# A second set of 16 value tiles of the last up projection made as seven block products

## The chip, the cores and the metric

The kernel runs on one core of one Trainium2 chip. The metric is the device time of one execution in microseconds; lower is better. Before the change three runs gave 2538.35 to 2538.91 us, with a median of 2538.77 us. One more execution was recorded by the profiler, and it took 2537.81 us; its span, from the first to the last instruction of the program, is 2535.6 us. All rows quoted below are of that execution, and times in rows are counted from the start of its span.

## The reference

The computation is a two-layer encoder on 16 learned meta tokens and 256 input tokens, with 2048 channels, in float32. Cut to what matters here, each layer is

```python
h = _rmsnorm(h_stream, norm_mix[i])
proj = h @ w_in[i]                                  # q, k, v, f, ga, gf
merged = g_attn * (attn @ w_attn_br[i]) + g_four * (fourier @ w_four[i])
h_stream = h_stream + merged @ w_out[i]

h2 = _rmsnorm(h_stream, norm_ffn[i])
up = h2 @ w_up[i]                                   # 2048 -> 2 * 5632
u_gate = _dwconv3_centred(up[..., :D_FF], w_conv[i], b_conv[i])
u_val = up[..., D_FF:]
h_stream = h_stream + (jax.nn.silu(u_gate) * u_val) @ w_down[i]
```

Only the 256 input tokens of the last layer are returned. The change is in the second half of layer two: in how a part of `u_val` is computed, and in the layer-two work that prepares its weights.

## The kernel before, in words

**Chunks.** Every weight matrix goes through TensorE (the matmul engine) in chunks of 512 KB: a tile of 128 partitions by 1024 float32 values, holding 4 blocks of 128 input channels by 256 output channels. A chunk is loaded by a transfer of the SP queue into a `raw` buffer (`load_raw`, line 244). It is then split in two parts that TensorE multiplies one after the other: ScalarE (ACT) makes the rounded part `wh` (line 280), and VectorE (DVE) makes the rest, `wl = raw - wh` (line 282). There are three `wh` and three `wl` buffers and four `raw` buffers; in the last stage every third load goes into one of two more (`raw5`), so that there are six. `next_split` keeps the splits two chunks ahead of TensorE. The chunks, in the order in which TensorE needs them, are one long list that is written out when the program is built.

**A group.** `group` takes the four chunks of a pair of channel tiles (2 x 128 output channels against 2048 input channels) and makes three matmuls for each block: `wh` with the rounded input, `wh` with the input's rest, `wl` with the rounded input (lines 343 to 345). For the value half of the last layer the two inputs are put side by side in one matmul of 512 columns, followed by one of 256 (lines 339 and 340, output `ps_uv`). For the gate half (`ps_ug`) the three matmuls have 258 columns. After every second block `step` is called, which lets work that waits in the background go on by one step. A chunk of a group has eight blocks and so four steps.

**The last stage.** In layer two the 22 pairs of the up projection are walked in the order `UP_ORDER`. For each pair comes the gate group (`ug`), its convolution and silu (`conv_gate`, lines 1210 to 1216), and then the value group (`uv`), whose result is put together on ACT and DVE (`v`, lines 1408 and 1409) and multiplied with the gate. Each activation of the first 40 channel tiles goes to the down projection, which is itself made as two sets (of 12 and 8 quarter products, `SETS`) of seven block products, with the scheme of Strassen and Winograd: sums of activation blocks times sums of weight blocks, seven products where the plain scheme has eight. The last four channel tiles (`t`) go through a plain down projection at the end.

**Products.** A product takes one chunk and makes six matmuls of 512 columns (line 1366, output `ps_p`). The generator `products` is drawn on between the chunks of the groups: the table `DUE` says how many products are to be done when t chunks of the last stage have been taken, with straight lines between its points. Between t = 8 and t = 152 it spreads 196 products. Their left operands (`opnd`) are sums of blocks, made on DVE and split on ACT and DVE by `make` and `split_unit` up to two units of three ahead; a finished product is handed out of PSUM by ACT or DVE (`hand_out`, `add`).

**One value set as products already.** Eight of the 22 pairs (`VPAIRS`, 16 channel tiles) have no `uv` group. Their values are made ahead by the first 56 products: block products of the scaled token stream with sums of the value weights. The results stand in `vR` with tokens on the partitions, and when such a pair's turn comes, four matmuls turn them (`ps_vr`, line 1399) and DVE multiplies them with the gate (line 1401).

**Sums of weights.** Four of the seven products need sums of weight blocks. For both the value set and the down projection these are made in layer one, between the feed-forward chunks, by `prepare`: transfers of the POOL queue bring weights into SBUF (`wi`), DVE adds (line 505), transfers of the POOL queue write the sums to DRAM (`fv`, `ft`, line 506). This runs at about 560 to 1260 us.

**What stands around the change.** The branch stage of layer two walks `BRANCH_ORDER` in two halves: gates `ga` and `gf`, the fourier and attention projections `s` and `a`, and after each half the eight groups of the output projection (`ps_o`). POOL's queue is in order, and its instruction for the root in the norm (`tok`, line 484) stands in it between that stage and the last one.

Of the kernel before, what the change touches and what calls it, by code (L numbers as in the profile page):

```python
# [16 lines left out]
P = 128  # L17
# [23 lines left out]
def _sets():  # L41
    up, prods, home, q0 = [], [], {}, 0
    for n in SETS:
        up += VFIRST if q0 == 0 else [q0 + i + j * n // 2 for i in range(n // 2) for j in range(2)]
        prods += _seven(1 + len(prods) // (7 * SETS[0]), q0, n)
        for k in range(n):
            home[2 * q0 + k], home[2 * q0 + n + k] = q0 + k, NQ + q0 + k
        q0 += n
    return up + list(range(NQ, FT // MG)), _seven(0, 0, NV) + prods, home
# [8 lines left out]
VPAIRS = [4, 10, 5, 11, 6, 7, 8, 9]  # L58
VFIRST = [0, 1, 2, 3] + VPAIRS[4:] + VPAIRS[:4]
UP_ORDER, PRODUCTS, HOME = _sets()  # L60
FIRSTS = [sum(SETS[:i]) for i in range(len(SETS))]
BEGIN = {(0, 0)} | {(i + 1, q) for i, q in enumerate(FIRSTS)}
END = {(0, NV - 1)} | {(i + 1, q + n - 1) for i, (q, n) in enumerate(zip(FIRSTS, SETS))}
DUE = ((0, 0), (8, 0), (34, 42), (50, 56), (64, 76), (66, 76), (112, 140), (128, 152), (130, 152), (144, 180), (150, 196), (152, 196))
# [94 lines left out]
def encoder_kernel(ctx, tc, xT, params, consts, bmat, cfold, csign, w_fl, w_f64c, w_in, w_abr, w_four, w_f64, w_out, w_up, w_down, w_vn, w_dn, w_dt, out):  # L159
# [8 lines left out]
    fv = dram.tile([4, NV, P, CW, MG * P], F32, name="fv")  # L168
# [38 lines left out]
    vprods = {0: w_vn[0, 0:NV], 1: w_vn[0, NV:KT], 2: w_vn[1, NV:KT], 3: fv[3], 4: fv[0], 5: fv[1], 6: fv[2]}  # L207
    pchunks = [((prods if s else vprods)[p][k], CW) for s, p, k in PRODUCTS]
# [7 lines left out]
    for key, chs in order:  # L216
        for j, ch in enumerate(chs):
# [4 lines left out]
            if n:  # L222
                mix[key, j] = n
                for s, p, k in PRODUCTS[done:done + n]:
                    if p in (3, 4, 5, 6):
                        summed[len(chunks)] = (s > 0, (3, 0, 1, 2)[p - 3], k)
                    chunks.append(pchunks[done])
                    done += 1
# [45 lines left out]
    def split_w(i, a, b, parts="hl"):  # L274
        if i not in splits:
            splits[i] = tuple(wp.tile([P, CW, MG * P], F32R, tag=t, name=f"{t}{i}") for t in ("wh", "wl"))
        h, lo = splits[i]
        r = raws[i]
# [11 lines left out]

    def step(force=False):
        for s in shadow:
# [211 lines left out]
    def prepare(pool):  # L504
# [5 lines left out]
        for f, wd, nq in ((fv, w_vn, NV), (ft, w_dn, NQ)):  # L510
            for k in range(nq):
                sums += [(wd[h, nq * e + k], (f, q, k)) for h, e, q in ((0, 0, 0), (1, 0, 2), (1, 1, 1), (0, 1, 3))]
# [10 lines left out]
        def sum_up(held, n, f, q, k):  # L523
# [5 lines left out]
            ready_sums.add((f is ft, q, k))  # L529

        for jobs, ahead, work in ((folds, 2, lambda h, n, to: fold(h, n, to)), (sums, 4, lambda h, n, to: sum_up(h, n, *to))):
            held = {}
            for n in range(len(jobs) + ahead):
# [8 lines left out]
                yield left  # L542

# [26 lines left out]

    xr = lambda lo: (lambda kt: (xH[:, kt, lo:T], xL[:, kt, lo:T]))
# [949 lines left out]
```

## Time and profile before

| what | value |
|---|---|
| median of the runs (range) | 2538.77 us (2538.35 to 2538.91) |
| profiled execution | 2537.81 us |
| its span | 2535.6 us |
| PE (TensorE matmul) busy | 2526.2 us, 100% of the span |
| DVE busy | 1952.5 us, 77% |
| ACT busy | 1317.9 us, 52% |
| POOL busy | 174.5 us, 7% |
| moved by DMA | 660.71 MB, mean 261 GB/s |

PE is the matmul row, and its busy time is the union of matmuls that overlap in the pipeline; what one costs is seen from the distance between starts. PEld is the load of weights into TensorE, which runs beside it. In a row of a group, the numbers behind the bar are the total and the mean duration of one instruction, then the idle time of the engine just before. In a row of a stretch of time there is, after its length, the busy time of each engine with the count of its instructions, then the granted TensorE clock, the busy share of the DMA engines and what they moved in GB/s. In a row of the timeline the first number is the start, the second the duration, and in brackets stands the idle time before it and what ended it. In a row of the DMA issues the last number is the median time from issue to landing.

### The profile page before, as it was taken

The numbers are of one execution on the slowest core, as the hardware profiler recorded it, in microseconds if no ns is written. First come the engines' busy times: TensorE is split into PE (matmuls) and PEld (weight loads), VectorE is DVE, ScalarE is ACT, GpSimd is POOL, SyncE is SP. The second block draws the span as 40 slices with busy tenths as digits, with TensorE's granted clock in tenths as the row PEclk, the third lists the DMA queues.
The fourth block names the chain that finished last, engine by engine and source line by source line (L and its number), as shares of the span: only waits on it lengthen the run. The fifth ranks groups of instructions, "written<-read, shape, count | busy, mean of one in ns | idle before, by whom it ended". The sixth has DMA issues, their size and how long they took to land.

```text
span 2535.6 us, 47924 instructions
## 1 busy us (share of the span) xinstructions
PE 2526.2 (100%) x18992; PEld 2445.7 (96%) x18992; DVE 1952.5 (77%) x3113; ACT 1317.9 (52%) x1893; POOL 174.5 (7%) x329
## 2 busy tenths in 40 slices
PE   9999999999999999999999999999999999999999
PEld 8999999999999999999999999999988999888987
DVE  7687866778878667888768787666778778777787
ACT  5455534454444334444445555444666566666565
POOL 0000000012212222222200000000000000000000
PEclk9999999999999999999999999999999999999999
DMA  6444555569999999999975645555578777877787
GB/s 238 164 157 161 188 181 186 186 240 372 388 336 377 398 381 366 389 382 379 386 267 187 194 142 187 193 195 195 184 252 268 246 251 252 264 262 265 240 269 256
DMA packets 186450, 660.71 MB, mean 261 GB/s; under 512 B 21217, under 2 KB 26465, under 8 KB 186225
## 3 DMA queue, kind: packets, MB, share of 16 engines
q1 hardware_dynamic: 143312, 504.51, 57.5%
q0 software_dynamic: 41472, 151.01, 15.8%
q8 instruction: 149, 2.44, 0.4%
q10 hardware_dynamic: 1440, 2.13, 0.2%
q14 instruction: 77, 0.62, 0.1%
HBM read 577.19 MB, written 77.59 MB: 258 GB/s over the span
## 4 chain that ended last, share of the span: by engine, by line
PE 99%; DMA 1%; DVE 0%; ACT 0%; SPq 0%; issue 0%; POOL 0%; ACTq 0%
PE ps_p L1366 11%; PE ps_ug L344 7%; PE ps_ug L345 7%; PE ps_ug L343 7%; PE ps_uv L339 4%; PE ps_d L343 4%; PE ps_uv L344 3%; PE ps_d L344 3%; PE ps_d L345 3%; PE ps_uv L345 3%; PE ps_uv L343 3%; PE ps_gf L344 2%; PE ps_ga L344 2%; PE ps_gf L345 2%; PE ps_o L344 2%; PE ps_o L345 2%
## 5 line engine op out<-in xcount | busy, mean ns | idle before, releaser
L282 DVE TENSOR_TENSOR wl<-raw,wh 128x1024 fp32r<-128x1024 f32 (+1 forms) x937 | 1129.2, 1217 | 445.9 <-ACT wh L280 437.7
L280 ACT CAST wh<-raw 128x1024 fp32r<-128x1024 f32 (+1 forms) x937 | 974.8, 1045 | 918.9 <-PE ps_ug L344 200.8
L344 PE MATMUL ps_ug<-xHL,wh 128*128 128x272 f32 (+1 forms) x1408 | 402.0, 286 | 0.0
L345 PE MATMUL ps_ug<-xHL,wl 128*128 128x272 f32 (+1 forms) x1408 | 401.4, 285 | 0.0
L343 PE MATMUL ps_ug<-xHL,wh 128*128 128x272 f32 (+1 forms) x1408 | 400.9, 285 | 0.0
L343 PEld LDWEIGHTS ps_ug<-xHL,wh 128*128 128x128 f32 x1408 | 264.6, 188 | 3.5
L344 PEld LDWEIGHTS ps_ug<-xHL,wh 128*128 128x128 f32 x1408 | 264.7, 188 | 3.3
L345 PEld LDWEIGHTS ps_ug<-xHL,wl 128*128 128x128 f32 x1408 | 264.7, 188 | 0.0
L344 PE MATMUL ps_uv<-xHL,wh 128*128 128x272 f32 x704 | 203.3, 289 | 0.0
L343 PE MATMUL ps_d<-gHL,wh 128*128 128x272 f32 x704 | 203.1, 288 | 0.0
L344 PE MATMUL ps_d<-gHL,wh 128*128 128x272 f32 x704 | 203.0, 288 | 0.0
L345 PE MATMUL ps_d<-gHL,wl 128*128 128x272 f32 x704 | 202.6, 288 | 0.0
L345 PE MATMUL ps_uv<-xHL,wl 128*128 128x272 f32 x704 | 202.6, 288 | 0.0
L343 PE MATMUL ps_uv<-xHL,wh 128*128 128x272 f32 x704 | 202.3, 287 | 0.0
L1366 PE MATMUL ps_p<-wh,opnd 128*128 128x512 f32 x688 | 188.7, 395 | 0.0
L339 PE MATMUL ps_uv<-xHL,wh 128*128 128x512 f32 x448 | 159.7, 395 | 0.0
L343 PE MATMUL ps_ga<-xHL,wh 128*128 128x272 f32 (+1 forms) x512 | 147.9, 289 | 0.0
L505 DVE TENSOR_TENSOR wi<-wi,wi 128x512 f32<-128x512 f32 x224 | 146.9, 685 | 0.0
L343 PE MATMUL ps_gf<-xHL,wh 128*128 128x272 f32 (+1 forms) x512 | 146.8, 287 | 0.0
L344 PE MATMUL ps_gf<-xHL,wh 128*128 128x272 f32 (+1 forms) x512 | 146.1, 285 | 0.0
L344 PE MATMUL ps_ga<-xHL,wh 128*128 128x272 f32 (+1 forms) x512 | 146.1, 285 | 0.0
L344 PE MATMUL ps_o<-mL,wh 128*128 128x272 f32 (+1 forms) x512 | 146.0, 285 | 0.0
(375 smaller groups left out, 6044.0 us busy)
## 6 DMA issues: line engine op xcount, KB each, us to landing
raw<-in_w_up SPq DMA_DIRECT2D x320, 512.0 KB, 5.3
raw<-in_w_in SPq DMA_DIRECT2D x191, 512.0 KB, 3.5
raw<-in_w_down SPq DMA_DIRECT2D x88, 512.0 KB, 7.0
wi<-in_w_dn POOLq DMA_DIRECT2D x80, 512.0 KB, 9.6
ft<-wi POOLq DMA_DIRECT2D x80, 512.0 KB, 8.0
raw<-ft SPq DMA_DIRECT2D x80, 512.0 KB, 4.5
raw<-in_w_out SPq DMA_DIRECT2D x64, 512.0 KB, 3.5
raw<-in_w_dn SPq DMA_DIRECT2D x60, 512.0 KB, 4.6
```

The lines of the kernel that those rows point to most:

```text
L280: nc.scalar.copy(h[:, a:b], r[:, a:b])
L282: nc.vector.tensor_tensor(lo[:, a:b], r[:, a:b], h[:, a:b].bitcast(F32), op=ALU.subtract)
L339: nc.tensor.matmul(o2, h[:, c, sl], ab, start=kt == 0, stop=False)
L343: nc.tensor.matmul(o, h[:, c, sl], a, start=kt == 0, stop=False)
L344: nc.tensor.matmul(o, h[:, c, sl], b, start=False, stop=False)
L345: nc.tensor.matmul(o, lo[:, c, sl], a, start=False, stop=kt == nk - 1)
L505: tt = lambda *v, **kw: tc.keep_in_program_order(nc.vector.tensor_tensor(*v, **kw))
L1366: nc.tensor.matmul(ps[h], x, w[:, 512 * h:512 * h + 512], start=fresh and (s_, q) in BEGIN and first, stop=(s_, q) in END and end, skip_gr ...
```

## The change

A second set of eight pairs (16 channel tiles) loses its `uv` groups and is made by 56 products, as the first one is. The sets are `VSETS`; products of the last stage become 252 instead of 196, over 120 chunks instead of 152, with a new `UP_ORDER` and a new `DUE`. The results of the second set get four buffers of their own (`late..`), which are used again for the split tail activations (`tails`).

The second set's weight sums aren't made by `prepare`. They are made by `weight_sums` in layer two, from the fifth entry of the first half of the branch stage on, one transfer for every 15 steps, 32 in all. For each of four sums and each of four pieces of 1 MB there is one transfer from DRAM to DRAM on POOL's queue that copies the first operand, and later one that adds the second operand to it in DRAM (`accum_op=ALU.add`). In the built program a copy has 16 rows of 16,384 values and an adding transfer 256 rows of 1,024 values. Ahead of each, POOL copies one column of the newest `wl` (`tick`), so that the transfer isn't issued before DVE has come that far. The four pieces of a sum are issued as copy, copy, add, copy, add, copy, add, add.

The memory set aside for the descriptors of POOL's transfers is set to 8192.

```diff
-DUE = ((0, 0), (8, 0), (34, 42), (50, 56), (64, 76), (66, 76), (112, 140), (128, 152), (130, 152), (144, 180), (150, 196), (152, 196))
+VSETS = ([8, 9, 10, 11, 4, 5, 6, 7], [14, 18, 15, 19, 12, 16, 13, 17])
+VPAIRS = {i: (s, c) for s, v in enumerate(VSETS) for c, i in enumerate(v)}
+PRODUCTS = [v for s in range(len(VSETS)) for v in _seven(s, 0, NV)] + [v for i, n in enumerate(SETS) for v in _seven(len(VSETS) + i, FIRSTS[i], n)]
+UP_ORDER = [0, 1, 2, 3] + [i for v in VSETS for i in v[4:] + v[:4]] + list(range(NQ, FT // MG))
+DUE = ((0, 0), (7, 0), (43, 96), (62, 112), (64, 112), (98, 196), (100, 196), (118, 252), (120, 252))
...
+    slow = [0, None, 0]
+
     def step(force=False):
+        if not force and slow[1] and slow[2]:
+            slow[0] -= 1
+            if slow[0] <= 0:
+                slow[0] = slow[2]
+                if next(slow[1], None) is None:
+                    slow[1] = None
...
+    def weight_sums():
+        rows = lambda ap: ap.rearrange("k p c m -> (k p) (c m)")
+
+        def issue(out_, s, **kw):
+            tick = small.tile([P, 1], F32, tag="tick", name="tick", bufs=1)
+            tc.keep_in_program_order(nc.gpsimd.tensor_copy(tick, st["wl"][:, 0, 0:1].bitcast(F32)))
+            tc.keep_in_program_order(nc.gpsimd.dma_start(out_, s, **kw))
+
+        for s_ in range(1, len(VSETS)):
+            dst = lambda q, j: rows(fv[s_][q, 2 * j:2 * j + 2])
+            w = lambda h, k, j: rows(w_vn[s_, h, NV * k + 2 * j:NV * k + 2 * j + 2])
+            kinds = ((0, lambda j: w(0, 0, j), lambda j: w(1, 0, j)),
+                     (1, lambda j: dst(0, j), lambda j: w(1, 1, j)),
+                     (2, lambda j: w(1, 1, j), lambda j: w(1, 0, j)),
+                     (3, lambda j: w(0, 1, j), lambda j: dst(1, j)))
+            for q, base, more in kinds:
+                for j in range(NV // 2 + 1):
+                    if j < NV // 2:
+                        issue(dst(q, j), base(j))
+                        yield 1
+                    if j:
+                        issue(dst(q, j - 1), more(j - 1), accum_op=ALU.add, max_dma_last_dim=4096)
+                        ready_sums.update((s_, q, 2 * j - 2 + k) for k in range(2))
+                        yield 1
...
-                for kind, i in BRANCH_ORDER[half]:
+                for n_, (kind, i) in enumerate(BRANCH_ORDER[half]):
+                    if last and (half or n_ >= 4):
+                        slow[2] = 15
...
-                vR = [own[:, a:a + 8].rearrange("p k t -> p (k t)") for a in (SETS[0], NQ + SETS[0] - (X1 - X0))]
+                flat = lambda t_: t_.rearrange("p k t -> p (k t)")
+                vR = [[[flat(own[:, a + 4 * c:a + 4 * c + 4]) for c in range(2)] for a in (SETS[0], NQ + SETS[0] - (X1 - X0))],
+                      [[flat(fp.tile([P, 4, SEQ], F32, tag=f"late{h}{c}", name="vR")) for c in range(2)] for h in range(2)]]
...
-                tH = fp.tile([P, NT, SEQ], F32R, name="tH")
-                tL = fp.tile([P, NT, SEQ], F32R, name="tL")
+                tails = []
...
+                            if not tails:
+                                tails += [fp.tile([P, NT, SEQ], F32R, tag=f"late0{c}", name=f"t{c}") for c in range(2)]
...
-    nc = _bacc.Bacc("TRN2", target_bir_lowering=False, num_devices=1)
+    nc = _bacc.Bacc("TRN2", target_bir_lowering=False, num_devices=1, dynamic_dma_scratch_size=8192)
```

More of the change, by code (lines that the diff above doesn't have):

```diff
@@ L167, in encoder_kernel @@
     ft = dram.tile([4, NQ, P, CW, MG * P], F32, name="ft")
[L168 removed]
+    fv = [dram.tile([4, NV, P, CW, MG * P], F32, name=f"fv{i}") for i in range(len(VSETS))]
     IN_F, IN_K, IN_V, IN_Q, IN_GA, IN_GF = 6, 4, 5, 0, 10, 18
@@ L1295, in encoder_kernel @@
                 made = {}
+                live = {(s_, c): (6, 8)[c] for s_ in range(len(VSETS)) for c in range(2)}
                 def make(s_, p, k, n):
-                    if s_ == 0:
+                    if s_ < len(VSETS):
                         s = vs[:, k:k + n]
@@ L1328, in encoder_kernel @@
                 whole, used = {(0, k) for k in range(NV)}, [0, 0]
+                vmade = sum(s_ < len(VSETS) for (s_, _), _ in units)
                 def make_ahead():
@@ L1332, in make_ahead @@
                         (s_, p), qs = units[used[1]]
-                        if not whole.issuperset((min(s_, 1), q) for q in qs):
+                        if not whole.issuperset((s_ >= len(VSETS), q) for q in qs):
                             break
```

66 lines of the change are left out of this document (32 added, 34 removed).

## The prediction

> **What bounds the kernel now.** I read the page first, then the waits of TensorE, then the busy time of each engine by stretches.
>
> ```profile
> span 2535.6 us, 47924 instructions
> PE 2526.2 (100%) x18992; PEld 2445.7 (96%) x18992; DVE 1952.5 (77%) x3113; ACT 1317.9 (52%) x1893; POOL 174.5 (7%) x329
> ...
> GB/s 238 164 157 161 188 181 186 186 240 372 388 336 377 398 381 366 389 382 379 386 267 187 194 142 187 193 195 195 184 252 268 246 251 252 264 262 265 240 269 256
> ...
> PE 99%; DMA 1%; DVE 0%; ACT 0%; SPq 0%; issue 0%; POOL 0%; ACTq 0%
> ```
>
> PE is busy all the time and makes up 99% of the chain that ended last. A busy PE could still be slow, so I asked what its matmuls waited for from 560 us to the end. The answer is one row:
>
> ```profile
> PE ps_uv L340 <- DVE wl L282: 0.3, 1, 0.3
> ```
>
> So the order of matmuls runs at TensorE's own pace; fewer columns are worth their whole time, and nothing else is, unless a feeder gets late. The feeders by stretch (layer-one preparation; the part of layer two's branch stage that the change uses; three parts of the last stage):
>
> ```profile
> core 0: us, PE busy (x) PEld busy (x) DVE busy (x) ACT busy (x) POOL busy (x), PEclk, DMA share, GB/s
> 560.00:1260.00 700.00, 700.00 (x5585) 700.00 (x5584) 553.85 (x848) 298.72 (x371) 144.80 (x272) 1.00 1.00 378
> 1495.00:1825.00 330.00, 330.00 (x2761) 330.00 (x2760) 234.37 (x410) 167.41 (x262) 0.00 (x0) 1.00 0.56 189
> ...
> 1875.00:2150.00 275.00, 275.00 (x1775) 249.81 (x1774) 219.89 (x288) 172.10 (x219) 0.00 (x0) 1.00 0.78 256
> 2150.00:2420.00 270.00, 270.00 (x1645) 240.89 (x1645) 207.33 (x259) 162.47 (x203) 0.00 (x0) 1.00 0.77 256
> 2420.00:2500.00 80.00, 80.00 (x424) 68.24 (x423) 70.77 (x90) 54.06 (x69) 0.00 (x0) 1.00 0.84 281
> ```
>
> The granted clock is 1.00 throughout. DVE is at 77 to 80% of the last stage, and at 88% (70.77 of 80) in its densest part, still without a wait of PE.
>
> **TensorE's part of the sum.** The timeline of PE around a product, a value chunk, and a set of transposes:
>
> ```profile
> 1870.18 1.09 PE L1366 MATMUL ps_p<-wh,opnd 128*128 128x512 f32 x4
> ...
> 1871.58 0.40 PE L339 MATMUL ps_uv<-xHL,wh 128*128 128x512 f32 x1
> ...
> 1874.37 0.39 PE L1366 MATMUL ps_p<-wh,xHL 128*128 128x512 f32 x1
> ```
>
> ```profile
> 1984.22 0.60 PE L1399 MATMUL ps_vr<-cst,act 128*128 128x128 f32 x4
> ...
> 1986.05 0.28 PE L343 MATMUL ps_ug<-xHL,wh 128*128 128x258 f32 x1
> ```
>
> A product takes 1871.58 - 1870.18 = 1.40 us. A value chunk takes 1874.37 - 1871.58 = 2.79 us. Four transposes and one product take 1986.05 - 1984.22 = 1.83 us, so the transposes cost 0.43. Removed: 8 pairs x 4 chunks x 2.79 = 89.3 us. Added: 56 x 1.40 = 78.4 us, and 8 x 0.43 = 3.4 us. The balance is -7.5 us; with 2.80 a value chunk it is -7.8. I take -7.6. In the built program TensorE's order is the same as before up to the eighth chunk of the last stage, so nothing else moves.
>
> **The splits and DVE.** The last stage has 372 chunks instead of 348 (24 more). A cast and its split, and how closely DVE can start one after the other:
>
> ```profile
> 1630.16 1.05 ACT L280 CAST wh<-raw 128x1024 fp32r<-128x1024 f32 x1 [1.81 <-PE ps_o L344]
> 1633.03 1.05 ACT L280 CAST wh<-raw 128x1024 fp32r<-128x1024 f32 x1 [1.83 <-PE ps_o L344]
> ```
>
> ```profile
> 1634.12 1.22 DVE L282 TENSOR_TENSOR wl<-raw,wh 128x1024 fp32r<-128x1024 f32 x1 [1.65 <-ACT wh L280]
> ```
>
> ```profile
> 1905.43 1.22 DVE L282 TENSOR_TENSOR wl<-raw,wh 128x1024 fp32r<-128x1024 f32 x1
> 1906.57 0.48 DVE L1214 SCALAR_TENSOR_TENSOR cv<-u,prm,cv 128x256 f32<-128x256 f32 x1
> 1906.96 1.22 DVE L282 TENSOR_TENSOR wl<-raw,wh 128x1024 fp32r<-128x1024 f32 x1
> ```
>
> A split holds DVE for 1.14 us (1906.57 - 1905.43), 0.08 less than its duration; I take 0.08 off every DVE duration. The other durations:
>
> ```profile
> L1289 DVE SCALAR_TENSOR_TENSOR res<-ps_p,sgn,res 128x512 f32<-128x512 f32 (+1 forms) x29 | 20.8, 735 | 0.2 <-PE ps_p L1442 0.2
> L1409 DVE TENSOR_TENSOR v<-v,ps_uv 128x256 f32<-128x256 f32 x28 | 11.6, 416 | 0.0
> L1224 DVE TENSOR_TENSOR opnd<-vs,opnd 128x384 fp32r<-128x384 f32 (+1 forms) x12 | 6.0, 508 | 0.0
> L1347 DVE TENSOR_TENSOR act<-act,ps_p 128x512 f32<-128x512 f32 x6 | 3.9, 682 | 0.0
> L1303 DVE TENSOR_TENSOR vs<-XT 128x384 f32<-128x384 f32 (+1 forms) x6 | 3.0, 512 | 2.6 <-ACT XT L1276 2.5
> ```
>
> DVE gains 24 splits (27.4 us), 12 operand splits and 12 block sums (24 x 0.43 = 10.3) and 6 hand-outs (6 x 0.60 = 3.6), and loses 16 additions of `v` (16 x 0.34 = 5.4): +36 us over some 702 us. The three rows of the last stage make 498 of 625 us, 80%; so DVE goes to about 85%. ACT gains about 27 us and stays under 70%. Neither saturates on the mean. Locally, the new table gives 2.5 to 3.1 products a chunk almost throughout, where before it was 1 to 2: runs of exactly three products go from 4 to 56, runs of two from 56 to 30. A gate chunk with three products takes PE 2.87 + 4.2 = 7.07 us (2.87 is the distance of the two casts above, one chunk of 258 columns). DVE needs four splits (4.56), a quarter of a pair's convolution and gate work (about 0.75 by rows of 0.34 to 0.40) and the products' own work (0.25 to 0.35 each): 6.1 to 6.4 us, 86 to 90%. The densest part before ran at 88% and cost nothing. I take 0.5 us for DVE, and as much for the start, where products now begin a chunk earlier and the one wait of PE already stands (0.3). If that cover is gone, see the second and third rival.
>
> **The wait in a run of products.** With three `wh` and `wl` buffers, a chunk's cast can begin only when the chunk three before it is used up. Cast to end of split is 1634.12 + 1.22 - 1633.03 = 2.31 us. After two products (2.80 us) and the two `wh` matmuls that come first in a gate chunk (0.24) the split part is needed, so 0.7 us are left. A third product adds 1.40 us of PE against 1.14 of DVE, so longer runs don't tighten it; another DVE instruction of 0.34 to 0.66 us at the wrong place nearly uses it up. This held 56 times before.
>
> **Weight sums.** In layer two a chunk has four steps and takes 2.87 us, so 15 steps are 10.8 us, and 32 transfers reach from about 1495 to 1840 us. First use is some 160 us into the last stage (28 chunks of 2.8 and 58 products of 1.4 us), so lateness of the sums themselves is hidden. What they can delay are the `raw` loads, and POOL. The landing times:
>
> ```profile
> raw<-in_w_down SPq DMA_DIRECT2D x88, 512.0 KB, 7.0
> ...
> raw<-in_w_out SPq DMA_DIRECT2D x64, 512.0 KB, 3.5
> ...
> wi<-in_w_vn POOLq DMA_DIRECT2D x32, 512.0 KB, 10.6
> fv<-wi POOLq DMA_DIRECT2D x32, 512.0 KB, 8.2
> ```
>
> A load has four chunks (11.5 us) less the 2.31 of the split, 9.2 us, to land; it takes 3.5. Then the split is ready 3.4 us early (two chunks, 5.74, less 2.31). So it may land in up to 12.6 us before PE waits. In layer one, with POOL's 512 KB transfers beside it at a DMA share of 1.00, `raw` loads came in 7.0 us, and in that stretch
>
> ```profile
> ACT wh L280 <- DMA raw<-in_w_up: 20.8, 12, 3.6
> ```
>
> ACT waited for loads 12 times and PE never. A piece of 64 KB on one engine, by the 3.5 us of a load that is 32 KB on each of 16, takes 7 us at most: 10.5 us with the load behind it. The extra stream, counted as the profile counts (each byte once), is 2 x 1.05 MB in 21.5 us = 98 GB/s on top of 189: 287, under the 378 that layer one sustained. I take 0. The DRAM-to-DRAM copy isn't in the trace: by rows it takes between 7 us (twice 3.5) and 21.2 (twice 10.6), and I take 10, since the DMA share here is nearer 0.56 than 1.00. An adding transfer is issued two or three slots (21.5 or 32 us) after its copy, so POOL wouldn't stand.
>
> **Smaller edits.** The 32 ticks read a `wl` buffer and hold it until POOL has come to them; three chunks (8.6 us) cover a free POOL. SP issues 24 loads more; a dense part asks for 4 chunks in 7.07 us, 297 GB/s, against 281 at a share of 0.84: about 0.89. Halved descriptor memory can touch only layer one's POOL transfers; their order is unchanged, and their sums are read from layer two on: 0, at worst what raises `raw` landing there, where 12 waits already occur.
>
> **Sum.** 2537.8 - 7.6 + 1.0 = 2531.2 us for the profiled execution, which stands 1.0 us under the median: **2532 us** on the median's scale.
>
> **Rivals.** A change under 0.2% (5.1 us) can't well be told from none, so the gain counts only if stalls stay under 2.5 us.
>
> *Part of it lost in runs of products.* There are 88 runs of two or more. At 0.07 us each, 6 us are lost: 2537. For it: the 0.7 us of room. Against it: 60 such runs without a wait.
>
> *The split chain becomes the bound (other side).* If in every run one DVE instruction stands in the way and PE waits 0.25 us, 22 us are lost: 2553. It decides from 0.15 us a run (12.7 us). For it: DVE at 86 to 90%, with three casts in a row that each wait for a buffer. Against it: 88% before at no cost.
>
> *DMA saturates in the branch stage (other side).* If every crossing of DRAM counts, a copy has two and an adding transfer three: 5 x 1.05 MB in 21.5 us is 244 GB/s, with 189 together 433. Against the 378 sustained at share 1.00, the 345 us would stretch by 15%, 50 us: 2581. For it: no row has a DRAM-to-DRAM or an adding transfer. Against it: landing may triple before PE waits. The Trainium skill, page "DMA: Bandwidth & Descriptors", section "Where 436 GB/s comes from", speaks against the change more strongly: it puts what a core gets from HBM at about 358 GB/s, by which 433 would, as an estimate, cost 72 us. The trace disagrees with that as a limit here: 378 over 700 us, and a slice of 398.
>
> *POOL stands at a late copy (other side).* At twice the layer-one latency each way (21.2 + 16.4 = 37.6 us) the eight adding transfers that follow their copy by two slots keep POOL 16 us; the next tick then holds a `wl` buffer about 7.5 us too long: 8 x 7.5 = 60 us, 2591. It decides from a landing of some 32 us.
>
> **Chances.** The forecast 0.50 (own range 2530 to 2534); part lost 0.23; split chain 0.15; DMA 0.08; POOL 0.04. Faster 0.50, same 0.23, slower 0.27. The range goes from 2530 (all of 7.8 and the present wait) to 2553, which leaves out DMA, POOL and the upper part of the split chain.
>
> **What would show it.** Right: the last stage shorter by some 7 us; no row of PE waiting for `wl` or `wh` over 1 us; DVE at 83 to 90%; `raw` loads of 1495 to 1840 us landing in under 10 us; copies landing in under 20. Wrong: PE waiting for `wl` after runs of products, ACT waiting for `raw` in the branch stage, or POOL waiting for DMA there with PE gaps behind.

## The result, and the profile after

The changed kernel took 2533.89 us (median of 22 runs, 2531.49 to 2540.80), and the kernel before, on the same chips, 2538.30 us (22 runs, 2537.27 to 2539.94). The ratio is 0.9986 with a 95% interval of 0.998 to 0.9993. So it is faster, by 4.4 us between the medians and by about 3.6 us by the ratio. That lies inside the predicted range and on the predicted side, but it is only between a half and two thirds of the 6.8 us that was forecast (2538.8 to 2532), and it is under the 0.2% that the prediction set as the bound of "faster". The runs of the changed kernel also differ by 9.3 us among themselves, those of the kernel before by 2.7.

The profiled execution of the changed kernel took 2533.09 us. Its page has these lines, in the order of those shown of before:

```profile
span 2531.2 us, 47928 instructions
PE 2517.9 (99%) x18848; PEld 2434.5 (96%) x18848; DVE 1985.4 (78%) x3151; ACT 1343.3 (53%) x1921; POOL 205.9 (8%) x393
...
PE 96%; DMA 2%; DVE 1%; ACT 1%; issue 0%; SPq 0%; POOL 0%; ACTq 0%; DVEq 0%
```

PE's busy time fell by 8.3 us and the span by 4.4, and 2% of the chain that ended last is now DMA, where before it was PE for 99%. To see where, I cut both executions at two places in the timeline of PE: the first matmul of layer two's branch stage (`ps_ga`) and the first one of the last stage (`ps_ug`). First the kernel before, then the changed one:

```profile
1444.37 0.28 PE L343 MATMUL ps_ga<-xHL,wh 128*128 128x258 f32 x1
...
1818.59 0.28 PE L343 MATMUL ps_ug<-xHL,wh 128*128 128x258 f32 x1
```

```profile
1445.22 0.28 PE L348 MATMUL ps_ga<-xHL,wh 128*128 128x258 f32 x1
...
1823.75 0.28 PE L348 MATMUL ps_ug<-xHL,wh 128*128 128x258 f32 x1
```

| part | before | after | difference |
|---|---|---|---|
| up to the branch stage of layer two | 1444.4 us | 1445.2 us | +0.9 |
| branch stage (difference of the two rows) | 374.2 us | 378.5 us | +4.3 |
| last stage (from the second row to the end of the span) | 717.0 us | 707.4 us | -9.6 |

The first part takes 1444 to 1448 us in the profiled executions of all kernels below, whether the change is in them or not, so 0.9 says nothing. The last stage gained 9.6 us, more than the 6.6 expected (7.6 less 1.0 of stalls). The branch stage lost 4.3 us, and that had been costed at nothing. The waits of PE from 560 us to the end of the changed kernel:

```profile
PE ps_gf L348 <- DVE so L1197: 1.5, 1, 1.5
PE ps_s L384 <- DVE wl L279: 0.9, 1, 0.9
PE ps_uv L345 <- DVE wl L279: 0.6, 2, 0.3
PE ps_ga L350 <- DVE wl L279: 0.4, 1, 0.4
```

Three of the four rows are in the branch stage (`ps_gf`, `ps_s`, `ps_ga`); the start of the last stage has the 0.6 us of `ps_uv`. The stretches of the prediction, with the same columns: the branch stage under the transfers, and two parts of the last stage.

```profile
1495.00:1825.00 330.00, 327.04 (x2726) 326.17 (x2725) 229.97 (x404) 164.55 (x258) 29.02 (x60) 1.00 0.88 279
...
1880.00:2500.00 620.00, 619.68 (x3723) 551.14 (x3722) 532.48 (x675) 414.80 (x519) 0.00 (x0) 1.00 0.84 283
2420.00:2500.00 80.00, 80.00 (x411) 67.91 (x410) 74.98 (x94) 55.80 (x70) 0.00 (x0) 1.00 0.90 311
```

In the branch stage the DMA share went from 0.56 to 0.88, the rate from 189 to 279 GB/s, and PE stood for 3.0 of 330 us in the records. In the last stage DVE is at 86% (532.48 of 620) and in its densest part at 94% (74.98 of 80), and PE is busy throughout.

So there are two questions. What in the weight sums cost 4.3 us? And where did the last stage find 3 us more than its sum of matmuls gives?

### The profile page after: what moved, and what is told of

Same layout as the page of the kernel before. It is cut to its first block, busy times and chain, and to the rows that moved or that the text cites. A ratio compares the mean times of both kernels' runs of the same rounds, so it can differ in the third digit from the quotient of the medians.

```text
span 2531.2 us, 47928 instructions
## 1 busy us (share of the span) xinstructions
PE 2517.9 (99%) x18848; PEld 2434.5 (96%) x18848; DVE 1985.4 (78%) x3151; ACT 1343.3 (53%) x1921; POOL 205.9 (8%) x393
## 4 chain that ended last, share of the span: by engine, by line
PE 96%; DMA 2%; DVE 1%; ACT 1%; issue 0%; SPq 0%; POOL 0%; ACTq 0%; DVEq 0%
PE ps_p L1403 14%; PE ps_ug L350 7%; PE ps_ug L349 7%; PE ps_ug L348 7%; PE ps_d L349 4%; PE ps_uv L349 4%; PE ps_d L348 3%; PE ps_uv L350 3%; PE ps_d L350 3%; PE ps_uv L348 3%; PE ps_o L349 2%; PE ps_gf L349 2%; PE ps_o L348 2%; PE ps_gf L348 2%; PE ps_o L350 2%; PE ps_gf L350 2%
## 5 line engine op out<-in xcount | busy, mean ns | idle before, releaser
L279 DVE TENSOR_TENSOR wl<-raw,wh 128x1024 fp32r<-128x1024 f32 (+1 forms) x961 | 1158.4, 1217 | 411.9 <-ACT wh L277 399.6
L277 ACT CAST wh<-raw 128x1024 fp32r<-128x1024 f32 (+1 forms) x961 | 999.8, 1045 | 901.7 <-PE ps_ug L349 213.3
L1403 PE MATMUL ps_p<-wh,opnd 128*128 128x512 f32 x816 | 222.8, 393 | 0.0
L1403 PEld LDWEIGHTS ps_p<-wh,opnd 128*128 128x128 f32 x816 | 148.4, 188 | 29.6 <-ACT wh L277 0.2
L348 PE MATMUL ps_gf<-xHL,wh 128*128 128x272 f32 (+1 forms) x512 | 146.8, 287 | 1.5 <-DVE so L1197 1.5
L350 PE MATMUL ps_ga<-xHL,wl 128*128 128x272 f32 (+1 forms) x512 | 146.1, 285 | 0.4 <-DVE wl L279 0.4
```

The source lines that it names most:

```text
L277: nc.scalar.copy(h[:, a:b], r[:, a:b])
L279: nc.vector.tensor_tensor(lo[:, a:b], r[:, a:b], h[:, a:b].bitcast(F32), op=ALU.subtract)
L348: nc.tensor.matmul(o, h[:, c, sl], a, start=kt == 0, stop=False)
L350: nc.tensor.matmul(o, lo[:, c, sl], a, start=False, stop=kt == nk - 1)
L1403: nc.tensor.matmul(ps[h], x, w[:, 512 * h:512 * h + 512], start=fresh and (s_, q) in BEGIN and first, stop=(s_, q) in END and end, skip_gr ...
```

## Experiments on the weight sums

The theory after the result: the weight sums make `raw` loads late in the branch stage. The rival was that the gain is lost elsewhere (ticks on POOL, the smaller descriptor memory, runs of products). Every run below is set against runs of the kernel before on the same chip (medians of 2538.2 to 2538.7 us). Stages are cut as above.

**No sums at all** (`e1_no_sums`). The second set reads plain weights where it would read sums, and nothing is transferred for them.

```diff
+vprods[1].update({p: w_vn[1, 1, 0:NV] for p in (3, 4, 5, 6)})
...
-slow[1] = weight_sums()
+ready_sums.update((1, q, k) for q in range(4) for k in range(NV))
```

> The 32 transfers and ticks of the weight sums in layer two are left out; the second set's sum products read plain weight tiles instead, so its values are wrong and every chunk, split and matmul stays. Theory A (the branch stage loses about 4 us to raw loads that land late beside the transfers, and the last stage keeps all of its gain): about 2529 us, branch stage back to 374 us, last stage 707, raw loads of 1550 to 1800 us landing in 3.5 us again, runs within 2 us of each other. Theory B (the loss stands in the runs of products, where loads and splits have less room): no better than 2532, and the last stage shows the waits.

2532.1 us (9 runs, 2530.68 to 2535.66), ratio 0.9976 [0.9967, 0.9986]. The branch stage is back at 374.2 us, so all 4.3 us come from the sums with their ticks. Its stretch under the transfers, where now there are none:

```profile
1495.00:1825.00 330.00, 330.00 (x2762) 330.00 (x2762) 234.32 (x409) 166.84 (x261) 0.00 (x0) 1.00 0.60 189
```

But the last stage took 710.9 us, 3.5 longer than with the sums, although its matmuls are the same in number and shape. So theory A was right about the branch stage and missed the total (2529), and theory B had the total (2532) but not the waits: PE waits in the last stage for 0.6 us, as in the changed kernel. That is taken up in the next section.

**Copies without additions** (`e3_copies_only`): the second operand is never added.

```diff
-issue(dst(q, j - 1), more(j - 1), accum_op=ALU.add, max_dma_last_dim=4096)
+pass
```

> The 16 adding transfers and their ticks are left out, the copies stay in their places; the sums are wrong. If the copies' 64 KB pieces cause the late loads: branch stage still 377 to 378 us, total 2532 to 2533. If the adding transfers do, or both on top of each other: branch stage near 374.5, total 2529 to 2530.

2528.74 us (5 runs, 2528.06 to 2529.05), ratio 0.9959 [0.9946, 0.9973]; branch stage 374.4 us, and no wait of PE in it. Its stretch:

```profile
1495.00:1825.00 330.00, 330.00 (x2761) 330.00 (x2760) 234.52 (x409) 166.80 (x261) 12.50 (x32) 1.00 0.71 239
```

So the copies by themselves, with half of the ticks, cost nothing. The spread of the runs is 1.0 us, where the changed kernel has 9.3.

**The additions as plain copies** (`e9_adds_as_copies`): the same 256 rows of 1,024 values, in the same places and as many bytes, but not added.

```diff
-issue(dst(q, j - 1), more(j - 1), accum_op=ALU.add, max_dma_last_dim=4096)
+issue(dst(q, j - 1), more(j - 1), max_dma_last_dim=4096)
```

> The 16 adding transfers of the changed kernel become plain copies of the same pieces (256 rows of 1,024 values), in the same places; the sums are wrong. If adding is what slows the loads beside it: these 16 land in 7 to 8 us instead of 11.9, the branch stage takes 374.5 us, total 2528 to 2529.5, runs within 1.5 us. If the number of transfers or the packets of 4 KB beside pieces of 64 KB do it: branch stage 377 to 379, total 2532 to 2534.

2528.86 us (5 runs, 2527.57 to 2531.75), ratio 0.9959 [0.9945, 0.9972]; branch stage 374.4 us.

```profile
1495.00:1825.00 330.00, 330.00 (x2760) 330.00 (x2760) 233.37 (x407) 167.11 (x262) 23.04 (x60) 1.00 0.81 282
```

The bytes that the profile counts are those of the changed kernel (282 and 279 GB/s), the number of transfers and of ticks is the same, and nothing is lost. What costs time is the adding. (Its runs spread by 4.2 us, not by the 1.5 expected.) How much more an adding transfer costs than a copy can be read from the packets of POOL's queue, from 1495 to 1850 us; the last number is the time that they took, as a share of 16 engines. The changed kernel, then this one:

```profile
q0 software_dynamic: 4776, 33.26, 36.9%
```

```profile
q0 software_dynamic: 4864, 33.56, 24.6%
```

With the copies alone (`e3_copies_only`) it is 11.9%. So the additions took 25.0%, and plain copies of the same pieces 12.7%: an adding transfer takes about twice the DMA time. (By the shares of the whole stretch, 0.71 with copies, 0.81 with plain copies for the additions and 0.88 with additions, it would be 1.7 times; but there the loads count as well, and without any such transfer that share differs by 0.04 between kernels, from 0.56 before to 0.60 in `e1_no_sums`.) The landing times go the same way. First the changed kernel, then this one; a row without KB is that of the copies of 16 rows, and the last number is the median from issue to landing:

```profile
fv<-in_w_vn POOLq DMA_DIRECT2D x12, 1024.0 KB, 11.9
...
fv<-in_w_vn POOLq DMA_DIRECT2D x12, 7.7
```

```profile
fv<-in_w_vn POOLq DMA_DIRECT2D x12, 1024.0 KB, 7.1
```

The Trainium skill, page "DMA: Bandwidth & Descriptors", section "Rules for kernel authors", says that an accumulating DMA reads its destination and writes it later; it gives no price. The traces agree that an addition is more work than the counted bytes show; three crossings of memory for a copy's two would be 1.5 times, and the packets took about twice.

What the additions do to the loads, in the DMA issues of 1495 to 1850 us: before, changed, and additions as copies.

```profile
raw<-in_w_out SPq DMA_DIRECT2D x32, 512.0 KB, 3.5
...
raw<-in_w_abr SPq DMA_DIRECT2D x16, 512.0 KB, 3.4
```

```profile
raw<-in_w_out SPq DMA_DIRECT2D x32, 512.0 KB, 6.4
...
raw<-in_w_abr SPq DMA_DIRECT2D x16, 512.0 KB, 7.0
```

```profile
raw<-in_w_out SPq DMA_DIRECT2D x32, 512.0 KB, 5.0
...
raw<-in_w_abr SPq DMA_DIRECT2D x16, 512.0 KB, 3.7
```

The medians go from 3.5 and 3.4 to 6.4 and 7.0 us in the changed kernel, about twice as long; of its single loads the slowest took 12.3 us (8.6 with the additions as copies). ACT then waits for `raw`, in the waits of the changed kernel over the same time:

```profile
ACT wh L277 <- DMA raw<-in_w_in: 23.7, 9, 5.3
...
ACT wh L277 <- DMA raw<-in_w_abr: 7.8, 3, 4.0
```

Most of these waits are covered by the splits made ahead. They reach PE around the chunks of the fourier projection `s`. In the kernel before, the timeline of ACT has there

```profile
1579.11 2.01 ACT L280 CAST wh<-raw 128x1024 fp32r<-128x1024 f32 x2 [0.60 <-ACT se L1163]
```

two casts back to back, because TensorE runs through the two chunks of an `s` in 4.0 us and not in twice 2.87. In the changed kernel the timeline of ACT reads

```profile
1584.41 1.05 ACT L277 CAST wh<-raw 128x1024 fp32r<-128x1024 f32 x1 [1.87 <-DMA raw<-in_w_in]
1589.47 1.05 ACT L277 CAST wh<-raw 128x1024 fp32r<-128x1024 f32 x1 [4.01 <-DMA raw<-in_w_abr]
1591.54 1.05 ACT L277 CAST wh<-raw 128x1024 fp32r<-128x1024 f32 x1 [1.01 <-DMA raw<-in_w_abr]
1595.65 1.05 ACT L277 CAST wh<-raw 128x1024 fp32r<-128x1024 f32 x1 [0.87 <-PE ps_a L350]
1598.40 1.05 ACT L277 CAST wh<-raw 128x1024 fp32r<-128x1024 f32 x1 [1.28 <-PE ps_a L349]
```

three loads late one after the other, and then the two chunks of the next `s`. Their loads (`raw<-fw`) were issued at 1584.47 and 1587.47 us, and the view of `raw` from 1584 to 1588 us has

```profile
DMA to landing us min/median/max: 10.8/11.0/11.1
```

so they landed at 1595.6 and 1598.3 us, and the casts follow within 0.1 us: they waited for these loads too, though the rows name PE. Beside them went the two adding transfers that end a sum, issued at 1577.32 and 1585.57 us. TensorE begins that `s` at 1598.30 us with no split left ahead, and stands within it and right behind it (timeline of PE):

```profile
1598.30 0.29 PE L383 MATMUL ps_s<-fr,wh 128*128 128x276 f32 x1
...
1600.76 0.33 PE L384 MATMUL ps_s<-fr,wl 128*128 128x138 f32 x1 [0.86 <-DVE wl L279]
...
1605.40 0.38 PE L348 MATMUL ps_gf<-xHL,wh 128*128 128x258 f32 x1 [1.46 <-DVE so L1197]
```

From its first matmul to the first of `ps_gf` this `s` takes 7.1 us; before, and with the additions as copies, it takes 4.0. That is 3.1 of the 4.3 us. Of the rest, 0.3 us lie in the `s` before it and 0.7 in a gate group at 1679 us, where the row of `ps_ga` stands. The same `s` takes 4.5 and 5.1 us in the two runs of the fine copies and 4.2 in the half pieces, both below. That the lost time lies there is read from these traces; no run changed those chunks alone.

**Copies of 256 rows** (`e2_fine_copies`, and once more on another chip as `e11_fine_again`). The copies go in pieces of 4 KB as the additions do, not in 16 pieces of 64 KB.

```diff
-issue(dst(q, j), base(j))
+issue(dst(q, j), base(j), max_dma_last_dim=4096)
```

> The 16 copies of the weight sums are cut in 256 rows of 1,024 values instead of 16 rows of 16,384, as the adding transfers are. If a raw load gets late because its packets stand behind pieces of 64 KB: landing in the branch stage falls from 6 to 9 us towards 5, the maximum under 9, and the time by 2 to 4 us to about 2530. If it is the amount that is moved: landing and time as in the changed kernel, within 1 us.

> The changed kernel with fine copies once more, beside the two others on the same chip: 2530.5 us, 0.3% under the kernel before.

2530.57 us (5 runs, 2528.46 to 2531.0), ratio 0.9966 [0.9953, 0.9978], and 2530.13 us (5 runs, 2529.25 to 2531.23), ratio 0.9966 [0.9953, 0.9978]; branch stage 375.1 and 375.5 us. The piece size brings back about three of the 4.3 us, though it moves no byte less (share 0.90). The loads landed hardly sooner than in the changed kernel (`raw<-in_w_out` in 5.9 us at the median for 6.4; the slowest load in 10.4, and in 10.7 on the other chip, where under 9 was expected). So the 64 KB pieces matter too, but only beside the additions: alone they cost nothing (`e3_copies_only`).

**Half pieces, twice as often** (`e10_halves`): on top of the fine copies, one transfer of 512 KB every 7 steps, and a copy is added to two pieces later.

```diff
-dst = lambda q, j: rows(fv[s_][q, 2 * j:2 * j + 2])
+dst = lambda q, j: rows(fv[s_][q, j:j + 1])
...
-for j in range(NV // 2 + 1):
+for j in range(NV + 2):
...
-issue(dst(q, j - 1), more(j - 1), accum_op=ALU.add, max_dma_last_dim=4096)
+issue(dst(q, j - 2), more(j - 2), accum_op=ALU.add, max_dma_last_dim=4096)
...
-slow[2] = 15
+slow[2] = 7
```

> All sums are made, by 64 transfers of 512 KB for every 7 steps instead of 32 of 1 MB for every 15, the copies also in rows of 1,024 values. If a long adding transfer is what a load stands behind: longest raw landing of the branch stage under 9 us, branch stage 374.5 us, total 2529, runs within 1.5 us. If the amount in the stage decides: as the kernel with fine copies, 2530.5. If more ticks hold wl buffers: slower than that.

2528.52 us (5 runs, 2527.71 to 2530.13), ratio 0.9960 [0.9948, 0.9973]; branch stage 375.5 us. This is the fastest version that makes all the sums. The total is the one expected (2529), but not for the reason given: the slowest load still took 10.6 us instead of under 9, `raw<-in_w_out` landed in 6.6 us at the median, and the branch stage is 1 us over 374.5. It is some 2 us ahead of the fine copies, but the intervals overlap, and the stages of the profiled executions are the same, so what these 2 us would be isn't seen. Its stretch has the highest share of all and still only 0.7 us of PE's time is missing in it:

```profile
1495.00:1825.00 330.00, 329.31 (x2751) 328.96 (x2751) 233.28 (x408) 167.37 (x261) 57.74 (x128) 1.00 0.93 287
```

So the mean share alone doesn't make loads late; how much comes at once may, but no run measured that by itself.

**A slower pace** (`e4_pace22`): 22 steps between transfers, not 15.

```diff
-slow[2] = 15
+slow[2] = 22
```

> One transfer for every 22 steps instead of 15 (15.8 us instead of 10.8), so that copies of 11 to 12 us and adding transfers of 8 us no longer overlap; they reach to some 2000 us, into the last stage. Theory A with overlap as its cause: branch stage 375 us, total about 2530, last stage up to 1 us longer. If each transfer alone delays a load: total 2533 as before. If the last stage can't bear them: over 2535.

2537.66 us (11 runs, 2534.08 to 2539.88), ratio 0.9993 [0.9984, 1.0002]. The branch stage fell to 374.9 us as wanted, but now the transfers reach to about 2000 us, beside the first products, and the last stage took 717.7 us. Its waits of PE from 1850 us on, and the stretch in which they lie (1850 to 2000 us):

```profile
PE ps_p L1403 <- ACT wh L277: 2.7, 3, 1.2
PE ps_ug L350 <- DVE wl L279: 1.7, 2, 1.2
PE ps_uv L345 <- DVE wl L279: 0.9, 2, 0.5
```

```profile
1850.00:2000.00 150.00, 146.74 (x792) 124.03 (x793) 119.99 (x141) 97.04 (x116) 16.05 (x20) 0.99 0.98 339
```

At a share of 0.98, PE loses 3.3 of these 150 us in the records, and the last stage is 10 us longer than in the changed kernel. A part of that is the clock: the 0.99 of the row comes from a dip of the granted clock, 0.86 from 1930 to 1942 us, which is worth 1.7 us. Where products run, the DMA share is 0.84 in the changed kernel without any such transfer (1880 to 2500 us, above), and the transfers on top of that cost these 10 us.

**The descriptor memory alone** (`e8_scratch`): only that edit, on the kernel before.

```diff
-nc = _bacc.Bacc("TRN2", target_bir_lowering=False, num_devices=1)
+nc = _bacc.Bacc("TRN2", target_bir_lowering=False, num_devices=1, dynamic_dma_scratch_size=8192)
```

> The kernel before with the memory for POOL's descriptors set to 8192 alone. The prediction's step: 0, 2538.4. If layer one's transfers suffer: slower, with raw loads of 560 to 1260 us landing later than 7 to 8 us and PE waiting there.

2539.25 us (10 runs, 2537.78 to 2540.26), ratio 1.0003 [0.9994, 1.0013], and the stages are those of before (374.2 and 717.0 us). It costs nothing there; what it does to the new transfers was not tried, since every version with them has it.

## Experiments on the last stage

`e1_no_sums` had 710.9 us in the last stage, the kernel with sums 707.4. The one thing that the sums leave behind there is a tile: `tick`, 4 bytes in each partition, for which 32 are set aside. It moves every tile that is allocated later by 32 bytes, the operands `opnd` of the products among them. In the kernel before, `opnd` begins at a multiple of 64 bytes in its partition, and `wh` and `wl` at 32 past one; in the changed kernel both are 32 past.

**The tile on the kernel before** (`e5_before_32`), and **36 bytes for the tick in the changed kernel** (`e6_after_64`), for which 64 are set aside, so that `opnd` is at a multiple of 64 again:

```diff
 # e5_before_32, after the pool `small` is made
+nc.gpsimd.memset(small.tile([P, 1], F32, tag="pad", name="pad", bufs=1), 0.0)
 # e6_after_64
-tick = small.tile([P, 1], F32, tag="tick", name="tick", bufs=1)
+tick = small.tile([P, 9], F32, tag="tick", name="tick", bufs=1)
...
```

> The kernel before, with one tile of 4 bytes a partition added to the small pool, as the tick of the changed kernel is. Nothing else changes but the place of all later tiles in SBUF: operand tiles of the products start at 32 instead of 0 modulo 64 bytes. Theory C (products ran at 1.39 instead of 1.40 us because of that place): matmuls of the products 227 instead of 234 ns apart, 2.5 us faster, about 2536. Theory D (they ran faster because they stand in longer runs, or for another reason): as before, 2538.4.

> The changed kernel with a tick tile of 36 instead of 4 bytes, so that the later tiles stand where they stood before (operands at 0 modulo 64 bytes); the same transfers. Theory C: matmuls of the products at 234 ns again, last stage 711 instead of 707.4 us, 3.4 us slower than the changed kernel, about 2537, so hardly any gain left. Theory D: as the changed kernel, 2533.5.

`e5_before_32`: 2536.28 us (11 runs, 2535.04 to 2540.53), ratio 0.9993 [0.9984, 1.0002]; last stage 714.7 us, 2.3 less than before. `e6_after_64`: 2538.92 us (11 runs, 2533.67 to 2540.53), ratio 0.9998 [0.9989, 1.0007]; last stage 711.5 us, 4.1 more than with the 4-byte tick, and the gain of the whole change is gone (its branch stage also took 6.4 us more than before's). The trace shows why the branch stage is even longer than the 378.5 us of the changed kernel. PE waits 3.0 us in the `s` at 1597 us, and right behind these waits the granted clock drops:

```profile
1602.00:1607.00 5.00, 5.00 (x30) 5.00 (x30) 4.90 (x12) 3.06 (x6) 0.00 (x0) 0.66 0.61 208
```

At 0.66 for 5 us it costs another 1.7 us; matmuls of 276 columns take 0.53 us there instead of 0.34.

Neither ratio is settled by itself, but the lengths of the stage go both ways with the place of the tiles.

**Only the operands moved** (`e12_operands_32`): `e1_no_sums` again, sums left out as there, with 4 bytes set aside just before `opnd` is allocated.

```diff
+if not made:
+    nc.gpsimd.memset(fp.tile([P, 1], F32, tag="pad", name="pad", bufs=1), 0.0)
```

> The kernel without the sums' transfers and ticks (plain weight tiles in their place, so the second set's values are wrong), and 4 bytes a partition allocated just ahead of the two operand tiles of the products: these two move from 0 to 32 modulo 64 bytes, every other tile stays. If the place of the operand tiles alone sets the products' pace: the products' matmuls 227 ns apart, last stage 707.4 instead of 710.9 us, total 2528.5 instead of 2532.1. If it is one of the other tiles that the tick moved along: 710.9 and 2532.

2528.68 us (5 runs, 2527.2 to 2532.51), ratio 0.9963 [0.9949, 0.9976], with 2532.1 for `e1_no_sums` (ratio 0.9976 [0.9967, 0.9986], so the two intervals overlap a little); last stage 707.2 us for 710.9. The groups of products in the last stage, `e1_no_sums` first, then this one:

```profile
L1404 PE MATMUL ps_p<-wh,opnd 128*128 128x512 f32 x816 | 225.2, 396 | 0.0
...
L1404 PE MATMUL ps_p<-wl,opnd 128*128 128x512 f32 x408 | 128.0, 394 | 0.0
...
L1404 PE MATMUL ps_p<-wh,xHL 128*128 128x512 f32 x192 | 52.7, 396 | 0.0
```

```profile
L1406 PE MATMUL ps_p<-wh,opnd 128*128 128x512 f32 x816 | 222.9, 393 | 0.0
...
L1406 PE MATMUL ps_p<-wl,opnd 128*128 128x512 f32 x408 | 126.3, 391 | 0.0
...
L1406 PE MATMUL ps_p<-wh,xHL 128*128 128x512 f32 x192 | 52.7, 396 | 0.0
```

The same 1224 matmuls with `opnd` take 4.0 us less (2.3 and 1.7), and those with `xHL`, whose place didn't change, the same to 0.1. That accounts for the whole difference of the stage (3.7 us). Where two of these matmuls follow each other directly, they now start 230.5 ns apart on average, not 233.9; the most frequent distance is 227 ns, where it was 234 to 235. So the 227 that the expectations speak of is not the distance of all of them.

**`wh` and `wl` moved as well** (`e7_wp_32`): on the kernel before, 4 bytes set aside ahead of their pool, so that they and `opnd` all move by 32 bytes, and their places relative to each other stay.

```diff
+pad = per.tile([P, 1], F32, name="pad")
+nc.gpsimd.memset(pad, 0.0)
```

> The kernel before, with 4 bytes a partition added behind the permanent tiles, so that the wh and wl buffers move to 0 modulo 64 bytes (the scaled input stays at 0) and the products' operands to 32. If a matmul runs faster when its two operands start at the same place modulo 64 bytes: the groups' matmuls of 258 and 272 columns come under 119 ns apart and the time falls by tens of us. If only the operand of the weight load matters: products gain 2.5 us as in the kernel with 4 bytes in the small pool, and the groups, whose weight load reads wh and wl, change by as much or lose it.

2542.13 us (11 runs, 2541.52 to 2545.4), ratio 1.0017 [1.0008, 1.0026]; last stage 719.9 us, 2.9 more than before, and branch stage 375.9 us, 1.7 more. The groups of the last stage that matter, before and then this kernel:

```profile
L345 PE MATMUL ps_ug<-xHL,wl 128*128 128x258 f32 x704 | 198.8, 282 | 0.0
L344 PE MATMUL ps_ug<-xHL,wh 128*128 128x258 f32 x704 | 198.8, 282 | 0.0
L343 PE MATMUL ps_ug<-xHL,wh 128*128 128x258 f32 x704 | 198.3, 282 | 0.0
L1366 PE MATMUL ps_p<-wh,opnd 128*128 128x512 f32 x688 | 188.7, 395 | 0.0
```

```profile
L343 PE MATMUL ps_ug<-xHL,wh 128*128 128x258 f32 x704 | 200.9, 285 | 0.0
L344 PE MATMUL ps_ug<-xHL,wh 128*128 128x258 f32 x704 | 199.2, 283 | 0.0
L345 PE MATMUL ps_ug<-xHL,wl 128*128 128x258 f32 x704 | 198.9, 283 | 0.0
L1368 PE MATMUL ps_p<-wh,opnd 128*128 128x512 f32 x688 | 188.8, 395 | 0.0
```

The products are back at the time of before, although `opnd` is where it was in `e5_before_32`. So the place of `opnd` alone doesn't decide, and with it the second expectation fell; in the runs so far the products are faster only where `opnd`, `wh` and `wl` all lie 32 past. And the gate groups became slower, though `xHL`, `wh` and `wl` now all lie at a multiple of 64, so the first expectation fell too: their three rows add up to 599.0 us, not 595.9, about the 2.9 us of the stage. Whether the place of `xHL` relative to `wh` is behind that wasn't separated.

## Why the prediction was right or wrong

All kernels together: the table gives the stages of the profiled execution and the ratio of the runs.

| kernel | branch stage, us | last stage, us | ratio [95%] |
|---|---|---|---|
| before | 374.2 | 717.0 | 1 |
| after | 378.5 | 707.4 | 0.9986 [0.998, 0.9993] |
| no sums | 374.2 | 710.9 | 0.9976 [0.9967, 0.9986] |
| no sums, operands moved by 32 bytes | 374.2 | 707.2 | 0.9963 [0.9949, 0.9976] |
| copies only | 374.4 | 707.4 | 0.9959 [0.9946, 0.9973] |
| additions as plain copies | 374.4 | 707.5 | 0.9959 [0.9945, 0.9972] |
| fine copies | 375.1 | 707.4 | 0.9966 [0.9953, 0.9978] |
| fine copies, again | 375.5 | 707.4 | 0.9966 [0.9953, 0.9978] |
| half pieces | 375.5 | 707.4 | 0.9960 [0.9948, 0.9973] |
| pace 22 | 374.9 | 717.7 | 0.9993 [0.9984, 1.0002] |
| after, operands back | 380.7 | 711.5 | 0.9998 [0.9989, 1.0007] |
| before, operands moved by the 4-byte tile | 374.4 | 714.7 | 0.9993 [0.9984, 1.0002] |
| before, `wh`, `wl` and operands moved | 375.9 | 719.9 | 1.0017 [1.0008, 1.0026] |
| before, descriptor memory alone | 374.2 | 717.0 | 1.0003 [0.9994, 1.0013] |

The forecast of 2532 was near to 2533.9 partly by luck: two things that it didn't contain, +4.3 and -3.5 us, nearly cancel.

- *TensorE's part of the sum, -7.6, and the stalls of DVE and of the start, +1.0.* Right in sum. With the operands in their old place and no sums, the last stage is 6.1 us shorter (`e1_no_sums`: 717.0 to 710.9); the two steps together said 6.6. Of the 1.0 us of stalls only 0.3 shows in the waits of PE, though, so TensorE's part was nearer to 6.4 than to 7.6 and the two errors cancel; what the missing 1.2 us are, no row says. DVE came to 86% (85% was worked out) and to 94% in the densest part, with no wait of PE there. The start has 0.6 us of waits, where 0.3 stood and 0.5 more was allowed.
- *Part of it lost in runs of products, and the split chain as the bound.* Neither happened: the last stage has no wait for `wl` or `wh` but those two of 0.3 us. DVE at 94% over 80 us still costs nothing, so that fear was too large.
- *Weight sums: "I take 0".* This is the step that failed, at +4.3 us in the profiled execution. Three numbers of it were wrong. It priced an adding transfer by the bytes that the profile counts; the rate came out as predicted (279 GB/s for 287), but the DMA time was about twice that of a copy. It let the sums on a `raw` load at 10.5 us at most; the slowest took 12.3, so the sign that loads land in under 10 us failed too. And it gave a load 12.6 us before PE waits, from the steady chunks of 2.87 us; the two chunks of an `s` take 4.0 us, and several late loads in a row use up the splits made ahead, so that PE lost 3.1 us in one `s` to loads that took 11.1 and 10.8 us, under that margin. The rows for this stood in the trace of before: a prediction that took the margin at `s` would have seen less room there.
- *DMA saturates in the branch stage.* The mechanism was right in kind: the additions do load the DMA beyond their counted bytes, and PE waits behind ACT for `raw`, as "what would show it" named under wrong. But its size was 50 us by the count of crossings, and the runs show 4. By that count 433 GB/s were asked for, and the stretch was not filled (share 0.88). By the 358 GB/s that the Trainium skill, page "DMA: Bandwidth & Descriptors", section "Where 436 GB/s comes from", gives a core from HBM, the estimate was 72 us; the trace disagrees with that as well.
- *POOL stands at a late copy.* It didn't: the copies landed in 7.7 us, nearer to the lower bound of 7 than to the 10 taken, and in the changed kernel POOL waits before a transfer only for the `wl` of its tick.
- *Ticks at nothing, halved descriptor memory at nothing.* Right as far as tried: with all ticks and plain copies the branch stage is 374.4 us (`e9_adds_as_copies`), and `e8_scratch` gives 1.0003 [0.9994, 1.0013].
- *What was missing.* The 4-byte `tick` moved the operands by 32 bytes, and the products became 3.5 us faster in all (710.9 to 707.4). Nothing in the prediction looked at the place of tiles. It is shown by moving `opnd` alone (`e12_operands_32`); why the place matters isn't known.
- *The chances.* The rule that the gain counts only "if stalls stay under 2.5 us" was sound: with the additions made harmless the same change gives 0.9959, clearly faster, and with them 0.9986. The wide spread of the changed kernel's runs fits with loads that come late by chance, since the kernels without additions spread by 1.0 to 5.3 us; and the clock adds to it. In 14 of its 22 runs the mean granted clock is 0.998 or 0.999, all those over 2534.2 us among them; in the kernel before, beside the experiments, it is so in 5 of 70, and in none of the 15 with fine copies or half pieces. `e6_after_64` shows such a drop right behind a wait of PE. But only one execution of each kernel is kept as a trace, and in the profiled one of `e9_adds_as_copies`, at 0.998, the drop stands in the first 75 us, so what lengthened the others is argued.

## What to carry to other kernels

The margin for background transfers is to be taken where chunks are shortest and loads come in rows, not from the steady groups, and an adding DRAM transfer is to be priced well above a copy of the same bytes (here about twice the DMA time); small pieces issued often (512 KB in 4 KB rows) cost the least time here, though the loads beside them landed no sooner at the median. When a change adds a small tile, look at which tiles move: compare the mean duration and the spacing of matmuls whose work didn't change. Cut the span at the same instruction in both traces before explaining a net difference: here it was the sum of a gain that was forecast, a gain that nobody had planned, and a loss.

## What the runs showed of the hardware that was not expected

- An adding transfer of 1 MB from DRAM to DRAM lands in 11.9 us, the same rows as a plain copy in 7.1, both beside loads at about 190 GB/s; where the source is itself a sum (`fv<-fv`), it is 10.8 and 8.0. Its packets take about twice the DMA time. A plain copy of 1 MB in 16 rows lands in 6.7 to 7.7 us.
- At nearly the same counted rate (279, 282 and 287 GB/s) the branch stage took 378.5, 374.4 and 375.5 us, with DMA shares of 0.88, 0.81 and 0.93: neither the rate nor the share tells by itself when loads come late.
- Matmuls of 512 columns that hold a block of `opnd` in TensorE and stream `wh` or `wl` through it start 230.5 ns apart on average, most often 227, when both lie 32 past a multiple of 64 bytes in their partitions, and 233.9 ns, most often 234 to 235, when `opnd` lies at a multiple (`e12_operands_32` against `e1_no_sums`). With `opnd` 32 past and `wh` and `wl` at a multiple it is 233.5 (`e7_wp_32`), as before the change (233.2). `opnd` with `wh` and `wl` all at a multiple of 64 wasn't tried, and matmuls with `xHL` don't show it, so it is no full rule.
- Right behind 3.0 us of waits within 4 us, TensorE's granted clock fell to 0.66 over 5 us, which cost another 1.7 us (`e6_after_64`); the changed kernel with 2.3 us of waits at the same place kept a clock of 1.00.
